# RWKV layers: loras ahead of the last keys, receptances and token products ahead of the block solution, values beside it, blocks written one by one

## The chip, the cores and the metric

The kernel runs on one core of one Trainium2 chip. The metric is the device time of an execution in microseconds (us); lower is better. The time before is the median of three runs. One further execution was taken by the hardware profiler, and all rows of a trace below are of that one.

The names of the engines in the rows: PE is TensorE (matrix products, and PEld its loads of weights), DVE is VectorE, ACT is ScalarE, POOL is GpSimd, SP is SyncE, which here does nothing but start the loads of weights. ACT and POOL also issue DMAs (transfers between the on-chip memory and DRAM).

## What is computed

A network of four layers and a second block on 256 tokens of width 1024, in float32. Each layer has a mixer between two SwiGLU parts. The mixers of layers 0 and 3 are RWKV time mixing, of layer 1 a Mamba2, of layer 2 an attention with a window. The change touches the two RWKV mixers alone. Cut to what matters:

```python
def rwkv7_time_mix(h, mu, w_rkv, w_o, w0, w1, w2, a0, a1, a2, g1, g2, ...):
    dx = token_shift(h) - h
    xr, xw, xk, xv, xa, xg = [h + dx * mu[j] for j in range(6)]
    r, k, v = xr @ w_rkv[0], xk @ w_rkv[1], xv @ w_rkv[2]
    w = -softplus(-(w0 + tanh(xw @ w1) @ w2)) - 0.5
    decay = exp(-exp(w))
    a = sigmoid(a0 + (xa @ a1) @ a2)
    # layer 3 alone: v += (v_first - v) * sigmoid(v0 + (xv @ v1) @ v2)
    g = sigmoid(xg @ g1) @ g2
    kk = heads(k * k_k); kk = kk / max(norm(kk), 1e-12)
    k = k * (1 + (a - 1) * k_a)
    ...
    def step(state, inp):          # 256 tokens, 16 heads of 64
        r_t, w_t, k_t, v_t, kk_t, a_t = inp
        sa = einsum('bhvk,bhk->bhv', state, -kk_t)
        state = state * w_t + sa (x) (kk_t * a_t) + v_t (x) k_t
        return state, einsum('bhvk,bhk->bhv', state, r_t)
    y = scan(step, ...);  y = group_norm(y)
    bonus = sum(rh * kh * r_k, axis=-1) * vh
    return ((y + bonus) * g) @ w_o
```

## The kernel before, in words

**Tiles.** The width of 1024 lies in eight tiles of 128 partitions (KT = 8), two heads in each. The tokens are cut into four chunks of 64. The recurrence over tokens is replaced by products in a chunk: within a chunk, each token's `sa` depends on those of the tokens before it, which is a triangular system, solved by blocks of 32 x 32. There are 2 blocks for each of 4 chunks and 16 heads: 128 blocks, one in each partition.

**The stages of an RWKV mixer** (`rwkv`, line 653), in the order in which they come: the keys (`pjrkv`), with the loras of decay and rate beside them (`lora_wa`, `lora_up`); then for each pair of tiles `ahead(k0)`, which is `directions` (the normed keys, `ss`, `KK`), `decay` (running sums `cs`) and `factors`. `factors` ends with the products `pd` of directions and keys, whose copy `tm` goes to DRAM as `dL`. `solve` reads the blocks back into `LT`, one block in a partition, inverts them in 31 steps of two DVE instructions each (`fs`, `LT`; lines 865 and 866), and sends the result by DRAM (`dTU`) into `T` and `U`. After that, lanes run: `inverse` (`px`, `pt`), `recur` (the states of one tile, chunk by chunk), and at the end the output product `rwo`.

The parts that the change moves: `receive(i)` is the receptance of a tile, a `whole` (line 695, one tile of output, eight matrix products over a weight of 512 KB, `raw`), multiplied into `R`; `values(k)` is the same for the values (`Vv`); `grams(k)` makes the products `pg` of a tile, masked by DVE into `GM`; `tokens(k)` turns a tile's data to token order (`tok`), makes the bonus (`rk`, `bo`) and the values in token order (`tokv`, `UV`); `gates` is the lora of the gate (`g1a`, `g1b`, `lgs`, then `g2a`, `g2b`).

**What sets the order.** Each part is a generator that yields now and then. `weave` (line 233) takes them round robin, one step each, and what they emit is the order of the instructions; each engine then runs its own in that order, and waits where one needs the result of another engine or a buffer. So a part that is woven in at another place moves on all engines. Before, these lines set it around the solution (`SOLVED` is 4, `VALUES` (2, 6)):

```python
weave([chain(ahead(0), ahead(4)), chain(repeat(None, 2), ahead(2), ahead(6)),
       chain(*(values(k) for k in range(VALUES[0]))), chain(repeat(None, 6), plain(0, xr))])
...
weave([solve(), fill, chain(repeat(None, SOLVED), gates()),
       chain(*(chain(grams(k), tokens(k)) for k in range(4)))])
```

`fill` holds the values 2 to 5 and receptances 0 to 3 in turn. The lanes then take receptances 4 to 7 and values 6 and 7 along, and `grams` and `tokens` of tiles 4 to 7. `plain(0, xr)` is the mix that receptances multiply, `plain(3, xv)` that of the values.

**Weights** come in the order of use through SP's queue into three buffers (`raw`), so a load waits until the third load before it has been used. The DMAs of `dL`, `dTU`, `T` and `U` are issued by ACT (`self.bounce`) and POOL.

## Time and profile before

| | us |
|---|---|
| median of 3 runs (3024.62 to 3029.52) | 3026.28 |
| profiled execution | 3033.78 |
| span of its trace | 3032.0 |

The span is the time from the first to the last instruction in the trace; the profiled execution lies 7.5 us above the median. A row of the page gives for each engine the time in which it was busy in this span; an engine that waits for another is not busy. Two mixers of the kind that is changed lie in the span, from about 220 to 480 us and from about 2030 to 2280 us with their output.

### The profile page before, as it was taken

The numbers are of one execution on the slowest core, as the hardware profiler recorded it, in microseconds if no ns is written. First come the engines' busy times: TensorE is split into PE (matmuls) and PEld (weight loads), VectorE is DVE, ScalarE is ACT, GpSimd is POOL, SyncE is SP. The second block draws the span as 40 slices with busy tenths as digits, with TensorE's granted clock in tenths as the row PEclk, the third lists the DMA queues.
The fourth block names the chain that finished last, engine by engine and source line by source line (L and its number), as shares of the span: only waits on it lengthen the run. The fifth ranks groups of instructions, "written<-read, shape, count | busy, mean of one in ns | idle before, by whom it ended". The sixth has DMA issues, their size and how long they took to land. (4 is left out here: it accounts for less than half of the span.)

```text
span 3032.0 us, 57166 instructions
## 1 busy us (share of the span) xinstructions
PE 2889.5 (95%) x23002; PEld 2729.8 (90%) x23002; DVE 2180.5 (72%) x3805; ACT 1553.4 (51%) x2697; POOL 77.1 (3%) x89
## 2 busy tenths in 40 slices
PE   7998799999998999999999999998799999999898
PEld 6997688999998989999988999996688999889898
DVE  8886425888788888888887888774536757566754
ACT  5546134545456765455466545444245446644543
POOL 0001100000001100000000000001000000000000
PEclk9999799999999999999999999999799999999999
DMA  9983313797884547888844897853314665544464
GB/s 323 337 312 89 96 60 103 258 305 268 302 271 160 161 154 232 285 286 280 296 150 143 310 311 250 296 198 95 90 55 127 210 181 181 174 145 126 155 186 133
DMA packets 185051, 613.36 MB, mean 202 GB/s; under 512 B 30353, under 2 KB 34321, under 8 KB 184786
## 3 DMA queue, kind: packets, MB, share of 16 engines
q1 hardware_dynamic: 168626, 595.49, 59.7%
q0 software_dynamic: 2816, 8.72, 0.9%
q10 hardware_dynamic: 13344, 5.51, 0.8%
q8 instruction: 180, 2.95, 0.4%
q14 instruction: 85, 0.70, 0.1%
HBM read 603.31 MB, written 6.32 MB: 201 GB/s over the span
## 5 line engine op out<-in xcount | busy, mean ns | idle before, releaser
L295 ACT ACTIVATE wh<-raw 128x1024 fp32r<-128x1024 f32 (+3 forms) x824 | 850.9, 1036 | 929.4 <-DMA raw<-in_wi 243.5
L374 DVE TENSOR_TENSOR wl<-raw,wh 128x1024 fp32r<-128x1024 f32 (+3 forms) x824 | 987.4, 1200 | 390.8 <-ACT wh L295 385.1
L383 PE MATMUL pjwi<-xl,wh 128*128 128x256 f32 x2568 | 722.3, 283 | 3.8 <-DVE xl L507 3.5
L382 PE MATMUL pjwi<-xh,wh 128*128 128x256 f32 x2568 | 716.2, 283 | 2.8 <-ACT xh L295 1.5
L384 PE MATMUL pjwi<-xh,wl 128*128 128x256 f32 x2568 | 716.4, 281 | 0.0
L383 PEld LDWEIGHTS pjwi<-xl,wh 128*128 128x128 f32 x2568 | 485.1, 189 | 6.0 <-DVE xl L507 5.8
L384 PEld LDWEIGHTS pjwi<-xh,wl 128*128 128x128 f32 x2568 | 486.1, 190 | 0.0
L382 PEld LDWEIGHTS pjwi<-xh,wh 128*128 128x128 f32 x2568 | 480.9, 189 | 3.6 <-ACT xh L295 1.9
L383 PE MATMUL pdwo<-gl,wh 128*128 128x256 f32 x1408 | 396.4, 282 | 0.0
L384 PE MATMUL pdwo<-gh,wl 128*128 128x256 f32 x1408 | 395.6, 281 | 0.0
L382 PE MATMUL pdwo<-gh,wh 128*128 128x256 f32 x1408 | 395.1, 281 | 0.0
L423 DVE SCALAR_TENSOR_TENSOR aring<-aring,cbc 128x1024 f32<-128x1024 f32 x286 | 343.5, 1221 | 2.7 <-DMA aring<-in_adaw 2.6
L382 PEld LDWEIGHTS pdwo<-gh,wh 128*128 128x128 f32 x1408 | 265.3, 188 | 0.0
L384 PEld LDWEIGHTS pdwo<-gh,wl 128*128 128x128 f32 x1408 | 265.2, 188 | 0.0
L383 PEld LDWEIGHTS pdwo<-gl,wh 128*128 128x128 f32 x1408 | 265.1, 188 | 0.0
L695 PE MATMUL whole<-mf,raw 128*128 128x256 f32 x512 | 129.7, 407 | 13.7 <-DMA raw<-in_rkv 13.4
L695 PEld LDWEIGHTS whole<-mf,raw 128*128 128x128 f32 x512 | 101.0, 203 | 36.6 <-DMA raw<-in_rkv 15.9
L383 PE MATMUL pjw2i<-xl,wh 128*128 128x256 f32 x416 | 119.1, 287 | 0.0
L384 PE MATMUL pjw2i<-xh,wl 128*128 128x256 f32 x416 | 118.1, 284 | 0.0
L382 PE MATMUL pjw2i<-xh,wh 128*128 128x256 f32 x416 | 117.3, 282 | 0.1
L382 PE MATMUL pjmbi<-xh,wh 128*128 128x256 f32 x352 | 101.8, 293 | 4.5 <-ACT shc L295 2.1
L383 PE MATMUL pjmbi<-xl,wh 128*128 128x256 f32 x352 | 101.9, 291 | 0.0
(526 smaller groups left out, 5681.2 us busy)
## 6 DMA issues: line engine op xcount, KB each, us to landing
raw<-in_wi SPq DMA_DIRECT2D x352, 512.0 KB, 4.7
aring<-in_adaw SPq DMA_DIRECT2D x286, 512.0 KB, 5.3
raw<-in_wo SPq DMA_DIRECT2D x128, 512.0 KB, 4.8
raw<-in_w2i SPq DMA_DIRECT2D x56, 512.0 KB, 4.1
raw<-in_wo SPq DMA_DIRECT2D x64, 384.0 KB, 4.5
raw<-in_rkv SPq DMA_DIRECT2D x48, 512.0 KB, 3.7
raw<-in_mbi SPq DMA_DIRECT2D x48, 512.0 KB, 3.7
raw<-in_fg SPq DMA_DIRECT2D x22, 512.0 KB, 4.3
```

Source lines behind the costliest of these rows:

```text
L295: ins = self.nc.scalar.activation(out, in_, func, **k)
L374: self.last = self.nc.vector.tensor_tensor(lo, src, hi.bitcast(F32), SUB)
L382: mm(out, a, xh[:parts, k, :], start=start, stop=False)
L383: mm(out, a, xl[:parts, k, :], start=False, stop=False)
L384: mm(out, b, xh[:parts, k, :], start=False, stop=stop)
L423: ins = nc.vector.scalar_tensor_tensor(raw, raw, 1.0, self.cbc, MUL, MUL, accum_out=m[:, b % 24:b % 24 + 1])
L695: mm(ps[:, :T], w[:, k * P:k * P + P], x[0][:, k, :], start=k == 0, stop=k == KT - 1)
```

## The change

It moves work between the stages and changes the way of the blocks through DRAM; the amount of matrix work is the same.

- The loras of decay and rate, in layer 3 also that of the values, are woven from the start of the last keys, before them in each round, and yield less often. The mix for the receptances (`xr`) is made beside the keys as well.
- `ahead` of all four pairs is woven together, each starting two rounds after the one before, and beside it stand values 0 and 1, receptances 0 to 3, and `grams` and `tokens` of tiles 0 to 3. `tokens` no longer needs the values: it copies the product `bo` over `rk` and keeps it.
- Beside the solution stand values 2 to 7, the gates' lora and a new part, `bonus(k)`, that makes `tokv`, `UV` and the bonus of tiles 0 to 3.
- The lanes take receptances 4 to 7 along, no values.
- `dL` is laid out by blocks. Each pair writes eight pieces (32 partitions, four blocks' rows of 128 bytes each), four from ACT and four from POOL, where it was two from ACT with rows of 1 KB. `LT` is read by two DMAs of 64 partitions (4 KB in a row), where it was eight, with rows of 128 bytes.

```diff
--- before.py
+++ after.py
@@ -23,9 +23,8 @@
 EARLY = 2
 QB = 8
 STAGGER = (0, 1, 2, 3)
-SOLVED = 4
-VALUES = (2, 6)
-BURSTS = 3
+VALUES = 2
+BURSTS = 1
 START = 6
 AHEAD = 7
 IDLE = (1, 1, 3, 1, 1, 1)
@@ -719,7 +718,8 @@
             for k in range(KT):
                 mm(ps[:, :T], w[:, k * P:k * P + P], h[:, k, :], start=k == 0, stop=False)
                 mm(ps[:, :T], ws[k // 4][:, k % 4 * P:k % 4 * P + P], dx[:, k, :], start=False, stop=k == KT - 1)
-                yield
+                if k % 2:
+                    yield
             act(t[:64], ps[:64, :T], AF.Tanh)
             act(t[64:], ps[64:, :T], AF.Copy)
             yield
@@ -744,7 +744,7 @@
                     ps = self.ax("up")
                     mm(ps[:, :T], w[r, k * P:k * P + P], t[0][r], start=True, stop=True)
                     act(dst(k), c8(ps[:, :T]), AF.Sigmoid, bias=self.p(bias, k))
-                if k % 2 or len(ups) > 1:
+                if k % 2:
                     yield
 
         def project(n, x, done):
@@ -771,7 +771,7 @@
         SC, rest = self.small("SC", 4 * KT, 1), self.small("rest", 8, 1)
         SC = SC.rearrange("p (k c) -> p k c", c=4)
         V.tensor_scalar(rest, self.p(f"k_a{j}", 0, 8), -1.0, 1.0, MUL, ADD)
-        dL = self.dp.tile([2 * KT, 64 * T + 64], F32, name=f"dL_{l}")
+        dL = self.dp.tile([2, 4, KT, 2, 32, 32], F32, name=f"dL_{l}")
         dTU = self.dp.tile([2, 2, 32, 2, 1024], F32, name=f"dTU_{l}")
         KK, IP = self.b8("KK"), self.b8("IP")
         b2 = lambda name: self.sp.tile([P, 512], F32, tag="b2", name=name, bufs=3)
@@ -808,6 +808,7 @@
             act(SC[:, sl, :3], sc, AF.Exp, scale=-DECAY)
             V.scalar_tensor_tensor(c8(sg)[:, :, 1:], c8(kk)[:, :, 1:], -1.0, c8(e)[:, :, :63], MUL, MUL)
             V.scalar_tensor_tensor(c8(sg)[:, :, 0], c8(kk)[:, :, 0], -1.0, first, MUL, MUL)
+            decayed.update(range(k0, k0 + 2))
             yield
 
         def factors(k0):
@@ -832,8 +833,11 @@
             yield
             tm = b2("tm")
             act(tm, pd, AF.Copy)
-            for h_, r in enumerate(H2):
-                self.bounce.dma_start(dL[2 * k0:2 * k0 + 4].rearrange("(k h) x -> h k x", h=2)[h_, :, :64 * T].rearrange("k (s c) -> s k c", c=T), pair(tm)[r])
+            for n in range(4):
+                h_, i = divmod(n, 2)
+                for d, k in enumerate(ks):
+                    queues[(n + d) % 2].dma_start(dL[k // 4, :, 2 * (k % 4) + h_, i].rearrange("c s t -> s c t"),
+                                                  c8(pair(tm)[32 * n:32 * n + 32, d])[:, :, 32 * i:32 * i + 32])
             factored.update(ks)
             yield
 
@@ -843,13 +847,10 @@
             L, Tm = LT[:, 0], LT[:, 1]
             t3 = Tm.rearrange("p (i j) -> p i j", j=32)
             l3 = L.rearrange("p (i j) -> p i j", j=32)
-            queues = self.bounce, nc.gpsimd
             for half in range(2):
                 while len(factored) < 4 * half + 4:
                     yield
-                for c in range(4):
-                    o = 64 * half + 16 * c
-                    queues[c % 2].dma_start(l3[o:o + 16], dL[8 * half:8 * half + 8].rearrange("q (b x) -> (q b) x", b=2)[:, :32 * T].rearrange("g (i x) -> g i x", x=T)[:, :, 64 * c:64 * c + 32])
+                queues[half].dma_start(L[64 * half:64 * half + 64], dL[half].rearrange("c g i s t -> (c g i) (s t)"))
             V.memset(Tm, 0.0)
             V.memset(Tm[:, 0:1024:33], 1.0)
             U.append(self.b8("U", F32, (P, 32, 64)))
@@ -894,17 +895,25 @@
             yield
 
 
-        Vv, valued = self.b8("Vv"), set()
+        Vv, valued, decayed, factored = self.b8("Vv"), set(), set(), set()
+        queues = self.bounce, nc.gpsimd
         self.table(TABLE_SIGM)
-        loras = [lora_wa(lwa), lora_up("wa2", (j,), P, lwa, [(H2[0], f"w0{j}", lambda k: c8(SG[:, k])), (H2[1], f"a0{j}", Aa)])]
-        weave([keys, chain(*loras), plain(3, xv)])
+        lows, ups = [lora_wa(lwa)], [lora_up("wa2", (j,), P, lwa, [(H2[0], f"w0{j}", lambda k: c8(SG[:, k])), (H2[1], f"a0{j}", Aa)])]
         if j:
-            finish(chain(lora("v1", (j - 1,), xv, 32, AF.Copy, lv), lora_up("v2", (j - 1,), 32, lv, [(slice(0, 32), "v0", lambda k: c8(Vv[:, k]))])))
+            lows.append(lora("v1", (j - 1,), xv, 32, AF.Copy, lv))
+            ups.append(lora_up("v2", (j - 1,), 32, lv, [(slice(0, 32), "v0", lambda k: c8(Vv[:, k]))]))
+        mixes = chain(plain(3, xv), plain(0, xr))
+        if j:
+            for _ in range(4):
+                next(mixes)
+        weave([chain(*lows, *ups), keys, mixes])
         self.table(TABLE_NORM)
         hc = lambda t, h_: t[:, 64 * h_:64 * h_ + 64]
-        received, factored, solved, ready, U, GMs, UVs = set(), set(), [], set(), [], {}, {}
+        received, solved, ready, U, GMs, UVs, bos = set(), [], set(), [], {}, {}, {}
 
         def receive(i, tag, steps=2):
+            while i not in decayed:
+                yield
             ps = yield from whole(0, i, xr, tag, steps)
             V.tensor_tensor(R[:, i], R[:, i], ps, MUL)
             received.add(i)
@@ -926,7 +935,6 @@
                 yield
 
         ahead = lambda k0: chain(directions(k0), decay(k0), factors(k0))
-        weave([chain(ahead(0), ahead(4)), chain(repeat(None, 2), ahead(2), ahead(6)), chain(*(values(k) for k in range(VALUES[0]))), chain(repeat(None, 6), plain(0, xr))])
         def inverse(k):
 
             while not solved:
@@ -949,20 +957,27 @@
 
         def tokens(k):
 
+            rk = self.b1("rk")
+            V.scalar_tensor_tensor(c8(rk), c8(R[:, k]), self.p(f"r_k{j}", k), K(k), MUL, MUL)
+            pt = self.ax("tok")
+            both = AK[k // 4][:, k % 4].rearrange("p c q t -> p (c q t)")
+            for c in range(4):
+                nc.tensor.transpose(pt[:, P * c:P * c + P], both[:, P * c:P * c + P], ident)
+            act(both, pt, AF.Copy)
+            yield
+
+            bo = self.ax("bo")
+            mm(bo[:, :T], blk, rk, start=True, stop=True)
+            bos[k] = rk
+            act(rk, bo[:, :T], AF.Copy)
+            yield
+
+        def bonus(k):
+
             half = k // 4
             top, bot = H2[half], H2[1 - half]
             while k not in valued:
                 yield
-            rk = self.b1("rk")
-            V.scalar_tensor_tensor(c8(rk), c8(R[:, k]), self.p(f"r_k{j}", k), K(k), MUL, MUL)
-            bo = self.ax("bo")
-            mm(bo[:, :T], blk, rk, start=True, stop=True)
-            pt = self.ax("tok")
-            both = AK[half][:, k % 4].rearrange("p c q t -> p (c q t)")
-            for c in range(4):
-                nc.tensor.transpose(pt[:, P * c:P * c + P], both[:, P * c:P * c + P], ident)
-            act(both, pt, AF.Copy)
-            yield
             if half not in UVs:
                 UVs[half] = self.b8("UV", F32, (P, 4, 512))
                 nc.gpsimd.memset(UVs[half][top], 0.0)
@@ -970,8 +985,7 @@
             for c in range(4):
                 mm(pv[bot, P * c:P * c + P], Vv[:, k, 64 * c:64 * c + 64], C["cen"], start=True, stop=True)
             act(UVs[half][bot, k % 4], pv[bot], AF.Copy)
-
-            V.tensor_tensor(Vv[:, k], bo[:, :T], Vv[:, k], MUL)
+            V.tensor_tensor(Vv[:, k], bos.pop(k), Vv[:, k], MUL)
             yield
 
         def recur(k, sts):
@@ -1066,9 +1080,11 @@
             self.table(TABLE_NORM)
             yield
 
-
-        fill = chain(*(p for k in range(4) for p in ([values(k + VALUES[0])] if k + VALUES[0] < VALUES[1] else []) + [receive(k, "mm")]))
-        weave([solve(), fill, chain(repeat(None, SOLVED), gates()), chain(*(chain(grams(k), tokens(k)) for k in range(4)))])
+        fill = chain(*(values(k) for k in range(VALUES)), *(receive(k, "mm") for k in range(4)))
+        weave([chain(repeat(None, k0), ahead(k0)) for k0 in range(0, KT, 2)] + [fill, chain(*(chain(grams(k), tokens(k)) for k in range(4)))])
+
+        fill = chain(*(values(k) for k in range(VALUES, KT)))
+        weave([solve(), fill, gates(), chain(*(bonus(k) for k in range(4)))])
         ST = self.b8("ST", F32, (P, 8, P))
         nc.gpsimd.memset(ST, 0.0)
         wg1, wg2 = self.get("g2a", (j,), 0, 1024, 128), self.get("g2b", (j,), 0, 1024, 32)
@@ -1092,11 +1108,8 @@
         sts = lambda n: (ST[:, 2 * n], ST[:, 2 * n + 1])
         lanes = [chain(repeat(None, s), inverse(n), recur(n, sts(n)), recur(n + 4, sts(n))) for n, s in enumerate(STAGGER)]
 
-        bursts = [receive(i, "ax", KT) for i in range(4, KT)]
-        for n, k in enumerate(range(VALUES[1], KT)):
-            bursts.insert(2 * n + 1, values(k, KT, "ax"))
-        rs = chain(*(chain(b, repeat(None, BURSTS - 2)) for b in bursts))
-        weave(lanes + [rs, chain(*(chain(grams(k), tokens(k), inverse(k)) for k in range(4, KT)))] + [closing(k) for k in range(0, KT, 2)] + [splits()])
+        rs = chain(*(chain(receive(i, "ax", KT), repeat(None, BURSTS)) for i in range(4, KT)))
+        weave(lanes + [rs, chain(*(chain(grams(k), tokens(k), bonus(k), inverse(k)) for k in range(4, KT)))] + [closing(k) for k in range(0, KT, 2)] + [splits()])
         m = self.mod(l, 1)
         finish(self.output(lambda i: ("rwo", (j, i)), Y, m))
 
```

The rows below are of the order of instructions in layer 0, before and after; a row is line, operation, result<-operands, shape and count.

PE before, from the third of four `pd` to the second `pg`; `whole` on `mf` are receptances and values, `lora` the gates' lora:

```order
L831 MATMUL pd<-SR,AK 64x64 x16
L695 MATMUL whole<-mf,raw 128x256 x10
L831 MATMUL pd<-SR,AK 64x64 x16
L733 MATMUL lora<-dx,raw 128x256 x8
L924 MATMUL pg<-SR,AK 128x128 x8
L733 MATMUL lora<-dx,raw 32x256 x8
L695 MATMUL whole<-mf,raw 128x256 x28
L959 MATMUL bo<-rk,cbase 128x256
L963 MATMUL tok<-cbase,AK 128x128 x4
L971 MATMUL tokv<-crw,Vv 64x128 x4
L924 MATMUL pg<-SR,AK 128x128 x8
```

The gates' lora stands among the first `pg`, 28 products of values and receptances ahead of the first `tok`. PE after, at the same place:

```order
L832 MATMUL pd<-SR,AK 64x64 x16
L694 MATMUL whole<-mf,raw 128x256 x16
L832 MATMUL pd<-SR,AK 64x64 x16
L933 MATMUL pg<-SR,AK 128x128 x8
L965 MATMUL tok<-cbase,AK 128x128 x4
L970 MATMUL bo<-rk,cbase 128x256
```

Now `pg`, `tok` and `bo` of a tile stand right behind the last `pd`, those of three more tiles behind them, with no lora among them.

PE after, in the second half of the solution and behind it, up to the first `pt` of the lanes (`pc` belongs to `recur`):

```order
L733 MATMUL lora<-dx,raw 32x256 x4
L986 MATMUL tokv<-crw,Vv 64x128 x4
L694 MATMUL whole<-mf,raw 128x256 x32
L1011 MATMUL pc<-UV,GM 64x64 x8
L948 MATMUL px<-T_3386,GM 32x32 x8
L694 MATMUL whole<-mf,raw 128x256 x8
L953 MATMUL pt<-U,X_3658 32x32 x8
```

The lora of the gates and the values stand now beside the solution and are done ahead of `px`, but for one `whole`.

ACT before, from the copy of the third pair's `pd` to the reads of the blocks (`DMA` is an issue, `ka` a factor of the next pair):

```order
L295 ACTIVATE tm<-pd 128x512
L295 ACTIVATE ka<-AK,rest,par 128x256
L836 DMA dL_2763<-tm 64x2x256 x2
L295 ACTIVATE ka<-AK,rest,par 128x256
L852 DMA LT<-dL_2763 16x32x32
L287 ACT_TABLE_LOAD
L295 ACTIVATE tm<-pd 128x512
L295 ACTIVATE Vv<-whole 128x256
L836 DMA dL_2763<-tm 64x2x256 x2
L295 ACTIVATE g1a<-lora 128x256
L852 DMA LT<-dL_2763 16x32x32 x2
```

Behind the last two stores stands one copy, then two reads.

ACT after, at the same place:

```order
L294 ACTIVATE ka<-AK,rest,par 128x256
L286 ACT_TABLE_LOAD
L294 ACTIVATE Vv<-whole 128x256
L294 ACTIVATE tm<-pd 128x512
L839 DMA dL_2759<-tm 32x4x32 x4
L294 ACTIVATE AK<-tok 128x512
L294 ACTIVATE rk<-bo 128x256
L294 ACTIVATE AK<-tok 128x512
L294 ACTIVATE rk<-bo 128x256
L853 DMA LT<-dL_2759 64x1024
```

Two stores have become four, and the read of half of the blocks stands behind the copies of two tiles' `tok` and `bo`.

## Rows read from the trace of the kernel before

**Rows 1.** The page: busy time of each engine, share of the span, instructions.

```profile
PE 2889.5 (95%) x23002; PEld 2729.8 (90%) x23002; DVE 2180.5 (72%) x3805; ACT 1553.4 (51%) x2697; POOL 77.1 (3%) x89
```

**Rows 2.** Stretches, layers 0, 3: length, PE, PEld, DVE, ACT, POOL busy, PEclk, DMA, GB/s.

```profile
265.80:308.70 42.90, 33.89 (x238) 26.15 (x236) 31.09 (x58) 21.45 (x43) 11.26 (x11) 0.93 0.36 99
308.70:323.60 14.90, 14.90 (x75) 11.46 (x76) 2.50 (x6) 3.90 (x8) 4.27 (x5) 0.98 0.56 156
323.60:353.50 29.90, 13.62 (x74) 11.21 (x73) 26.82 (x74) 4.06 (x7) 0.56 (x1) 0.77 0.28 87
353.50:376.00 22.50, 22.50 (x106) 18.07 (x103) 4.46 (x9) 4.00 (x8) 3.81 (x5) 0.54 0.34 74
376.00:476.40 100.40, 100.40 (x905) 81.88 (x904) 32.36 (x78) 40.01 (x112) 2.88 (x3) 0.95 0.17 52
...
2069.00:2112.50 43.50, 34.64 (x238) 25.76 (x237) 32.68 (x66) 23.38 (x47) 12.78 (x9) 0.92 0.38 100
2112.50:2127.10 14.60, 14.60 (x75) 11.22 (x76) 2.47 (x6) 3.36 (x6) 1.27 (x2) 1.00 0.61 144
2127.10:2158.90 31.80, 15.52 (x69) 12.78 (x68) 27.78 (x77) 3.58 (x5) 1.71 (x3) 0.68 0.28 90
2158.90:2176.30 17.40, 16.97 (x111) 13.72 (x109) 6.24 (x14) 4.21 (x8) 4.95 (x7) 0.80 0.46 110
2176.30:2276.00 99.70, 99.70 (x884) 81.56 (x884) 34.70 (x84) 38.39 (x106) 1.80 (x1) 0.93 0.17 53
```

**Rows 3.** Timeline of PE: start, length, work, in brackets idle time before and its end.

```profile
294.08 1.13 PE L695 MATMUL whole<-mf,raw 128*128 128x256 f32 x4 [2.71 <-DMA raw<-in_rkv]
...
304.35 2.43 PE L695 MATMUL whole<-mf,raw 128*128 128x256 f32 x8 [3.68 <-DMA raw<-in_rkv]
```

**Rows 4.** Groups of DVE, 323.6 to 353.5: busy, mean ns | idle time before.

```profile
L865 DVE TENSOR_TENSOR fs<-LT 128x31 f32<-128x31 f32 (+15 forms) x31 | 10.6, 342 | 1.0
L866 DVE TENSOR_TENSOR LT<-LT,fs 128x31 f32<-128x31 f32 (+15 forms) x31 | 10.6, 341 | 0.9
L374 DVE TENSOR_TENSOR wl<-raw,wh 128x1024 fp32r<-128x1024 f32 (+1 forms) x2 | 2.4, 1212 | 0.0
...
L925 DVE TENSOR_TENSOR GM<-pg,crw 128x512 f32<-128x512 f32 x2 | 1.4, 683 | 0.0
L869 DVE COPY LT<-LT 128x1024 f32<-128x1024 f32 x1 | 1.1, 1054 | 0.0
...
L974 DVE TENSOR_TENSOR Vv<-bo,Vv 128x256 f32<-128x256 f32 x1 | 0.4, 425 | 1.3 <-PE tokv L971 1.3
```

**Rows 5.** Timeline of PE: a `whole` at low clock, then work at full clock.

```profile
370.82 5.29 PE L695 MATMUL whole<-mf,raw 128*128 128x256 f32 x16
...
2167.28 1.74 PE L924 MATMUL pg<-SR,AK 64*128 64x128 f32 x16
...
2170.15 0.66 PE L963 MATMUL tok<-cbase,AK 128*128 128x128 f32 x4 [0.23 <-DVE GM L925]
2170.74 1.09 PE L971 MATMUL tokv<-crw,Vv 128*64 128x128 f32 x8
2171.75 0.69 PE L940 MATMUL px<-T,GM 32*32 32x32 f32 x16
2172.63 3.72 PE L695 MATMUL whole<-mf,raw 128*128 128x256 f32 x16
```

**Rows 6.** Tile views of `tm` (first two rows) and `dL`: min/median/max, ns of an issue, us to landing.

```profile
L836 ACTq DMA_DIRECT2D dL<-tm x16: 582/597/667, 277.1 to 2113.8; - x16
...
DMA to landing us min/median/max: 2.4/2.5/4.8
...
DMA to landing us min/median/max: 2.2/3.6/5.5
```

**Rows 7.** Timeline of POOL: the issue that reads T.

```profile
355.24 0.82 POOL L877 DMA_DIRECT2D T<-dTU  x1
```

**Rows 8.** DMA issues from 300 to 370: KB each, median us from issue to landing.

```profile
T<-dTU POOLq DMA_DIRECT2D x1, 128.0 KB, 4.5
```

## The prediction

> **What bounds the kernel now.** I read the page first: over the whole span TensorE (PE) is busy 95% of the time, the vector engine (DVE) 72%, the scalar engine (ACT) 51% [rows 1]. By that alone a change of order could win little; but the change touches only the two RWKV layers, and there the share is another. So I cut the two stretches into stages, at the instructions that end them (the timeline gives the marks): **A** from the first `ss` to the last `pd` (directions, decay, factors), **B** from there to the first step of `solve`, **C** the solution until the copy of `LT` has ended, **D** from there to the first `pt` of the lanes, **E** the lanes until `rwo` begins. In [rows 2] five rows are layer 0, five layer 3; the second column is the length of the stage, the third PE's busy time.
>
> In A PE is busy 33.9 of 42.9 us, in C 13.6 of 29.9; in layer 3 34.6 of 43.5 and 15.5 of 31.8. PE is thus idle for some 25 us a layer. In D it is busy throughout but at a granted clock of 0.54 (0.80 in layer 3), so that its work there takes nearly double. Only E is bound by PE, at 0.95 and 0.93. Next, the reasons, from PE's timeline: within A it waits for a key or receptance weight (`raw<-in_rkv`) 2.71 us at 294 and 3.68 at 304 [rows 3]. C is bound by DVE: its 31 steps are 10.6 + 10.6 us, the copy 1.1 [rows 4], of 26.8 busy.
>
> **The change, stage by stage.** The total of the matrix work stays; what changes is beside which other work it stands.
>
> *A.* Here DVE is busy 31.1 and ACT 21.5 of 42.9 us [rows 2], so neither fills it; the weights' waits and the chain through DVE do. After, the `g1a` and `g1b` loads stand behind ten rkv loads, not between them, so they hold no raw buffer during A, and the receptances' weights come in time. The order has 55 products of `whole` in place of 50 in this stage (one `whole`, a tile of output, is eight products, one for each tile of the input). A product is two records of the trace; a `whole`, 16 records, is 3.72 us at full clock [rows 5], 0.46 a product; I take 0.44, as they lie close to each other here. The sum is PE's busy time plus 5 x 0.44: 33.9 + 2.2 = 36.1 and 34.6 + 2.2 = 36.8, so -6.8 and -6.7. The two waits for weights are 6.4 us in layer 0, which is nearly this. DVE loses the receptances' mixes to the phase of the keys (there PE is the busy one) and gains two `R` products and four `rk`; it stays near 30, under 36.
>
> *B.* 14.9 and 14.6 us now: the gate loras and a product, all PE. They go to C. In their place stand four heads of `grams` and `tokens`: `pg` 1.74, `tok` 0.66 [rows 5] and `bo`, one product, 0.46, so 4 x 2.86 = 11.4, and one `GM` of DVE, 0.68 [rows 4], behind it: 12.1. The other chain of B is the way of the blocks: the copy `tm`, taken like an issue at 0.6, four issues on ACT of 0.6, landing 2.5 [rows 6], the read's issue 0.6 and its landing. That read of `dL` is new in form (rows of 4 KB, 64 partitions). The landings that bound it are the stores' 2.5 and the longest of `dL`, 5.5, which is a present read in pieces of 128 bytes, since the stores end at 4.8 [rows 6]: 8.6 to 11.6 us with it, in both cases below 12.1. So B is 12.1: -2.8 and -2.5.
>
> The new stores write pieces of 128 bytes where the old wrote 1 KB. The trace has for 128-byte pieces up to those 5.5 us, in reads, against 2.5 for the stores [rows 6]. If they land like those reads, the chain is 11.6 to 14.6 us and B at worst 14.6, 2.5 over my value; I take 2.5 us, the landing of stores, and keep the other for the upper end. The Trainium skill ("DMA: Bandwidth & Descriptors", Specifications) says that below 512 bytes a transfer falls under line rate, since the engine reads, modifies and writes. By that rule the stores would come under the dearer case, and the sum be -42 instead of -47.
>
> *C.* The steps and the copy stay: 21.2 + 1.1. Between them stood 4.5 us of other DVE work (26.8 less 22.3); in the order after stand four `Vv` products of 0.42, a `GM` of 0.68, two `lgs` like `Vv` and a split of a weight, 1.21 [rows 4]: 4.4. Of the idle time, 29.9 - 26.8 = 3.1, 1.9 is ahead of the steps themselves [rows 4] and stays. So 28.6, -1.3; layer 3, whose values bring more for DVE, I put at 30.8, -1.0. What PE gets here must fit: `tokv` 4 x 1.09 = 4.4 [rows 5], 16 lora products 7.4, 39 products of `whole` 17.2, together 29 us at full clock, as long as the stage; the 6 us in which D waits for T are the reserve. This is the cover for the moved work: if PE stands at half clock there (now 0.77, 0.68), the last values end up to 25 us later, in front of `px`.
>
> *D.* Now 22.5 and 17.4: T is read 1.7 us after the copy's end [rows 7] and lands after 4.5 [rows 8], at 359.7, but PE is still at half clock in `grams`, `tokens` and products, and `px` stands behind these. After, only `pc` and one `whole` stand there. 1.7 + 4.5 + `px` 0.7 and the `whole` at low clock, 5.3 us [rows 5], are 12.2: -10.3 and -5.2.
>
> *E.* Values 6 and 7 leave the lanes: two `whole`s of 3.7 [rows 5], and PE is busy throughout: -7.4 in each layer.
>
> *ACT and POOL.* Instead of 8 stores and 4 reads ACT issues 16 stores and a read, POOL the other 16 stores. One issue is 0.6 us [rows 6]. Nothing, if it falls into ACT's idle half of A; 8 x 0.6 = 4.8 if each of eight more lies in the chain from `tm` to `ka` of the next pair. I take 2 for each layer, the middle, as ACT idles half of A.
>
> **Sum.** Layer 0: -6.8 - 2.8 - 1.3 - 10.3 - 7.4 = -28.6. Layer 3: -6.7 - 2.5 - 1.0 - 5.2 - 7.4 = -22.8. Plus 4: -47.4. The profiled execution took 3033.78 us (its span 3032.0), 7.5 above the median of 3026.28; against it 2986.4, on the median 2979.
>
> **Rivals.**
>
> *The lanes don't shrink.* For it: in E the chain from `px` over `pt` to the states passes between DVE and PE in each lane, and DVE and ACT are busy 32 and 40 of 100 us. Against: PE has no idle time there. If both `whole`s merely filled gaps, 14.8 comes back: 2994.
>
> *PE stays cold.* Between C's work and `px` PE has only `pc` for some 6 us; after the idle stretches of C, 16 us in all, it was granted 0.54 in D. If E's first 22.5 us run so (0.54 for 0.95), some 10 us come back in each layer: about 3000. For it: D now. Against: only 6 us, with `pc` in it. The Trainium skill ("TensorE: Matmul & The Clock Gate", Part 1) says that idleness throttles the clock and sustained work releases it; D agrees, with its 0.54.
>
> *The stores hold ACT up: slower.* After, most stores of `dL` wait, by the order, for a DMA issued some eight DMAs earlier, weight loads included, and behind them on ACT stand `SR`, `ka` and `sq` of the next pairs, for which DVE and PE wait. If each waits x us, A is 21.5 + 12x (ACT's busy time and its stores in A), 23.4 + 12x in layer 3, and the chain of B (0.6 + 4x + 2.5 + 0.6 + some 4) is 4x - 4.4 longer than 12.1. Set against A's 36.1 and 36.8 and the mean gain of 25.7 per layer, it decides from 16x - 18.4 = 25.7, x = 2.75. At the median landing of `dL`, 3.6 [rows 6], a layer is some 13 us longer than now, 3053. For it: 2.75 lies within the landings. Against: eight DMAs earlier is mostly long landed by then.
>
> **Numbers.** My forecast has 0.58 and its own range, 2960 to 2995; the lanes' rival 0.13, the cold PE 0.13, the stores 0.16, of which 0.06 for small waits that leave it within 0.2% (6 us, about what a measurement can tell) and 0.10 for slower. So faster 0.84, same 0.06, slower 0.10. The low end: no issue costs (-4), the `whole` after `px` at full clock (5.29 to 3.72, twice: -3), E at full clock (0.05 and 0.07 of 100 us: -12): 2960. The high end: E gains nothing (+14.8), eight issues in the chain (+5.6), the read of `dL` in B 2.5 late in each layer (+5), and C 3 us longer for late products (+6): 3010. Below lies 0.04, above the stores' 0.16.
>
> **What would show it.** Right: no wait for `raw<-in_rkv` in A, which ends about 36 us after its start; the first step follows the last `pd` by about 12; C is filled with PE at a clock near 1; `px` follows the copy by 6 to 7. Wrong: dL's stores on ACT far apart, in front of idle DVE and PE; a solution that waits for `LT` after the `GM` are done; the values' `whole`s in front of `px`; lanes as long as before with idle PE.

## The result and the profile after

| | before | after |
|---|---|---|
| median, us | 3025.45 (4 runs, 3021.96 to 3029.52) | 3044.6 (4 runs, 3042.72 to 3046.63) |
| ratio, 95% interval | | 1.0063 [1.0045, 1.008] |
| profiled execution, us | 3033.78 | 3042.72 |

The change made the kernel slower by 0.6%; 2979 was forecast. The profiled execution of before lies 8.3 us above its median, that of after 1.9 below, so the two traces show only 8.9 us of the 19.2 between the medians. What is said of sizes below goes by the medians of the experiments where there is one.

The page of after, the line that answers to [rows 1]:

```profile
PE 2907.3 (96%) x23002; PEld 2740.7 (90%) x23002; DVE 2176.8 (72%) x3805; ACT 1557.4 (51%) x2713; POOL 88.9 (3%) x115
```

PE has as many instructions as before and is busy 17.8 us longer: the same work at a lower granted clock, over the whole span 0.963 of the full one, before 0.970. The stretches of after are cut at the same marks A to E as [rows 2], and a sixth, F, goes from the first `pjrwo` to the last. Columns: length; busy time of PE, PEld, DVE, ACT, POOL (x: instructions); PEclk, the granted clock as a share of the full one; DMA share; GB/s. Layer 0 comes first:

```profile
271.40:306.20 34.80, 32.62 (x248) 26.01 (x246) 25.34 (x46) 21.89 (x43) 14.44 (x19) 1.00 0.42 114
306.20:316.30 10.10, 10.10 (x89) 8.62 (x88) 5.51 (x10) 3.21 (x7) 5.63 (x8) 1.00 0.31 80
316.30:347.50 31.20, 30.09 (x158) 23.47 (x156) 25.63 (x71) 9.25 (x17) 3.96 (x6) 1.00 0.36 106
347.50:365.30 17.80, 7.58 (x37) 6.02 (x38) 1.21 (x1) 1.36 (x5) 5.27 (x6) 0.62 0.65 200
365.30:465.60 100.30, 100.30 (x831) 79.42 (x830) 31.91 (x77) 39.15 (x110) 0.00 (x0) 0.83 0.13 38
465.60:519.60 54.00, 50.65 (x341) 43.06 (x340) 24.13 (x51) 21.33 (x47) 0.00 (x0) 0.83 0.33 107
...
2078.60:2113.70 35.10, 32.64 (x248) 26.04 (x246) 26.83 (x53) 21.20 (x40) 13.51 (x17) 1.00 0.40 110
2113.70:2123.40 9.70, 9.70 (x83) 8.22 (x84) 6.01 (x12) 3.21 (x7) 6.44 (x8) 1.00 0.31 68
2123.40:2155.50 32.10, 30.19 (x152) 23.28 (x151) 26.86 (x78) 8.39 (x14) 3.68 (x6) 1.00 0.43 126
2155.50:2171.20 15.70, 8.63 (x45) 6.92 (x45) 4.57 (x11) 0.65 (x2) 4.73 (x5) 0.57 0.62 180
2171.20:2271.70 100.50, 100.50 (x832) 79.66 (x831) 31.91 (x77) 39.17 (x110) 0.00 (x0) 0.83 0.14 42
2271.70:2329.50 57.80, 55.08 (x340) 47.23 (x340) 23.00 (x45) 21.80 (x46) 0.00 (x0) 0.73 0.28 88
```

A to D are shorter in both layers. The loss is in E and F, which must be read together, since the order now sets the first `pjrwo` earlier among the lanes' products. Before they were 145.4 us (376.0 to 521.4) and 143.9 (2176.3 to 2320.2; the E of [rows 2] ends 3.3 us ahead of layer 3's first `pjrwo`); now 154.3 and 158.3, with two `whole`s less in each. The clock tells where: 0.83 in E, 0.83 and 0.73 in F, where before it was 0.95 and 0.93 [rows 2] in E. E and F as one stretch, before, layers 0 and 3:

```profile
376.00:521.40 145.40, 143.98 (x1208) 119.99 (x1208) 56.40 (x128) 60.07 (x154) 2.88 (x3) 0.93 0.24 75
2176.30:2320.20 143.90, 143.24 (x1208) 119.32 (x1208) 57.80 (x129) 60.66 (x153) 1.80 (x1) 0.93 0.23 72
```

And after:

```profile
365.30:519.60 154.30, 150.95 (x1171) 122.49 (x1170) 56.03 (x128) 60.49 (x156) 0.00 (x0) 0.83 0.20 62
2171.20:2329.50 158.30, 155.58 (x1170) 126.89 (x1170) 54.91 (x122) 60.98 (x155) 0.00 (x0) 0.80 0.19 59
```

The length times the clock, an estimate of the length at full clock, is 135 and 134 us before and 128 and 127 after: some 7 us less in each layer, as much as two `whole`s. So the work did leave E and F, and the lower clock more than ate it.

Two smaller losses lie ahead of A. Layer 3's keys with their loras, from the first `lora` to the first `ss`, take 53.0 us, before 47.3; and from the last `pdwo` to the first `lora` it is 10.9 and 6.9 us, before 5.8 and 5.0. DVE's timeline of after at the start of layer 0 (start, length, work, idle time ahead):

```profile
223.18 1.23 DVE L373 TENSOR_TENSOR wl<-raw,wh 128x1024 fp32r<-128x1024 f32 x1 [2.20 <-ACT wh L294]
224.78 0.69 DVE L717 TENSOR_TENSOR wmu<-raw,par 128x512 f32<-128x512 f32 x1 [0.38 <-DMA raw<-in_wa]
225.39 0.48 DVE L574 SCALAR_TENSOR_TENSOR xT<-pdwo,mod,xT 128x256 f32<-128x256 f32 x1
```

The last update of the residual (`xT`), on which the norm waits, now stands behind `wmu`, the scaled weight of the first lora, and `wmu` behind that weight's load; in the order of before it stands ahead of it. But `wmu` waits for its load for 0.38 us and takes 0.69, about 1 us of the 5.1 in layer 0; where the rest arises is not shown.

### The profile page after: what moved, and what is told of

The parts are those of the page before. It is cut to its first block, busy times and chain, and to the rows that moved or that the text cites. A ratio compares the mean times of both kernels' runs of the same rounds, so it can differ in the third digit from the quotient of the medians.

```text
span 3040.9 us, 57272 instructions
## 1 busy us (share of the span) xinstructions
PE 2907.3 (96%) x23002; PEld 2740.7 (90%) x23002; DVE 2176.8 (72%) x3805; ACT 1557.4 (51%) x2713; POOL 88.9 (3%) x115
```

## The experiments

A first theory: six `whole`s had kept PE's clock up in the lanes; the last now ends at 401 us (the expectation below has 404), before at 442, and PE then falls to half clock. The rival: lanes and output are paced by their own chain. Four runs. Before, run again beside all the experiments, had medians from 3023.26 to 3025.47 us, so that their medians can be set against that of after.

**Values 6 and 7 back in the lanes** (in all diffs below "-" is after, where not said otherwise):

```diff
-        fill = chain(*(values(k) for k in range(VALUES, KT)))
+        fill = chain(*(values(k) for k in range(VALUES, KT - 2)))
...
+        for n, k in enumerate(range(KT - 2, KT)):
+            bursts.insert(2 * n + 1, values(k, KT, "ax"))
```

> After, with the whole products of values 6 and 7 put back among the receptances in the lanes, at the places they had before. Clock theory: the lanes and the output product are 8.9 us longer than before in layer 0 and 14.4 in layer 3 since the last whole ends at 404 us, not at 444, and PE then falls to half clock; with six wholes again the granted clock from 430 to 490 us is near that of before (1.00 and 0.83 in two windows of 30 us, 0.71 and 0.66 after) and the time falls by some 23 us, to 3018 to 3025. Rival, that the lanes and the output are paced by their own chain of small products and weights, whatever else PE does: 3040 to 3048.

Measured 3043.29 (ratio to before 1.0056 [1.0037, 1.0075]): no change from after. With all six `whole`s in the lanes the clock fell all the same, to 0.51 from 437 to 488 us. The theory falls in this form. Lanes and output (E and F) became 10.4 us longer in both layers together, but stage D became 11.8 and 10.9 us (17.8 and 15.7 in after), of which more below.

**Products that do nothing, in place of the values**:

```diff
+        def warm():
+            ps = self.ax("warm")
+            for k in range(KT):
+                mm(ps[:, :T], blk, self.xT[:, k, :], start=k == 0, stop=k == KT - 1)
+            yield
...
+            bursts.insert(2 * n + 1, warm())
```

> After, with two bursts of eight more matrix products (a constant matrix times the residual, 128x256 each, result not used) at the two places in the lanes from which values 6 and 7 were taken; nothing else is changed, no load, no vector work. Clock theory: more work makes it faster: the clock stays up as before, and the lanes and the output lose 15 to 23 us, 3022 to 3030. Rival 1, lanes bound by PE's work: 7.4 us more in each layer, 3059. Rival 2, lanes paced by their own chain: no change, 3042 to 3048.

Measured 3053.97 (1.0078 [1.0054, 1.0102]): 9.4 us more than after, for 14.8 of work at 3.7 a burst, with overlapping intervals. In its trace E and F are 166.6 and 162.8 us at clocks of 0.81 and 0.82, 16.8 more than in after in all. So early work in the lanes did not bring the clock back; whether it costs two thirds of its length or all of it is not clear.

**Receptances farther apart** (`BURSTS` 4 for 1).

> After, with four idle rounds behind each receptance in the lanes where it was one, so that the four wholes lie farther apart and end later; work and loads are the same. Clock theory: half clock begins later, and the time falls by some 5 to 12 us, 3033 to 3040, unless the gaps between the wholes are now long enough for the clock to fall in them. Rival, own chain: tiles 4 to 7 get their receptances later and the lanes end later, 3045 to 3060.

Measured 3038.92 (1.0044 [1.0026, 1.0062]); 5.7 us less than after, with overlapping intervals: not clear.

**Loras as before**:

```diff
-        weave([chain(*lows, *ups), keys, mixes])
+        weave([keys, chain(*lows, *ups), chain(plain(3, xv), plain(0, xr))])
+        if j:
+            finish(chain(lora("v1", ...), lora_up("v2", ...)))
```

> After, with the loras woven as before (behind the keys in each round, a yield for each product, layer 3's lora of the values behind the keys); the rest of the change stays. Theory: in the order after, the first scaling of the lora weight (wmu) stands in DVE's row ahead of the last update of the residual, and waits for a weight; the norm, and all of the layer, starts 5.1 us later in layer 0 and 1.9 in layer 3, and layer 3's keys with both loras are 5.9 us longer. All three come back: 3029 to 3035. Rival, the gaps are the weights' loads themselves, in whatever order: 3042 to 3048.

Measured 3031.7 (1.0016 [0.9997, 1.0035]), 12.9 less than after. In its trace layer 3's keys are 47.2 us and the way to its first `lora` is 5.0, as before, and so in all later runs with the loras as before (47.2 to 48.0, 5.0 to 5.1). In layer 0 that way was 5.7 here, but between 6.7 and 10.9 us in most others with either order; how much of the 12.9 stands there is not shown.

**A new theory of the lanes.** The order has 32 groups of the chain's product `pc<-r,U` in a layer, one for each of eight tiles and four chunks. In before 24 stand ahead of the last `px` and 8 behind it, in after 26 and 6. (Counts in the expectations below were summed wrongly: 22 for before and 20 for one yield less are both 24; 18 for two chains is 15, and 18 for one yield less again is 21.) The reason is in the diff: `tokens` and `bonus` together yield once more than the old `tokens`, and tiles 4 to 7 go through `grams`, `tokens`, `bonus`, `inverse` one after the other, so the last tile comes four rounds of the weave later. Its recurrence then runs at the end with little beside it.

**One yield less for tiles 4 to 7**:

```diff
             act(rk, bo[:, :T], AF.Copy)
-            yield
+            if k < 4:
+                yield
```

> After, with one yield less in each of the tiles 4 to 7 of the lanes: tokens goes on into bonus in the same round of the weave, as the undivided tokens did before. No instruction is added or removed, only the order of the lanes moves: the last px stands behind 20 chain products r,U pairs fewer or more as before (22 groups ahead of it in before, 26 in after, 20 here). New theory, the serial part of tiles 4 to 7 (grams, tokens, bonus, inverse, one tile after the other) sets the pace, and its extra round per tile puts the last px four chain steps later, so that the last tile's recurrence runs alone at the end, at half clock: the lanes with the output get back to 145 and 144 us or less, -9 to -16 and -14 to -21: 3008 to 3022. Rival, the missing wholes and the clock: 3040 to 3048.

Measured 3013.6 (0.9954 [0.9933, 0.9974]): 31 us less than after, by one line that adds or removes no instruction. The order has 24 groups ahead of the last `px`.

**The converse on the kernel before** ("-" is nothing here; a line is added behind `tokens`' last yield):

```diff
             yield
+            if k >= 4:
+                yield
```

> The kernel before, with one empty yield more at the end of tokens for tiles 4 to 7, and nothing else. The order then has 26 chain groups ahead of the last px, as after has, with the six wholes where they were. Theory of the extra round: the lanes with the output are 9 to 20 us longer in each layer, 3040 to 3055. Rival, the clock kept by the wholes: they are all there, so no change, 3020 to 3030.

Measured 3047.55 (1.0079 [1.0065, 1.0093]), 23.7 more than before (3023.82 beside it), with 26 groups ahead of the last `px`. Both lines point the same way. PE's timeline of after, rows of the chain around the last `px` (start, length, work; four records of `pc<-r,U` are a group):

```profile
451.44 0.68 PE L1016 MATMUL pc<-r,U 64*64 64x64 f32 x4
456.94 0.69 PE L1016 MATMUL pc<-r,U 64*64 64x64 f32 x4
461.49 0.69 PE L1016 MATMUL pc<-r,U 64*64 64x64 f32 x4
463.15 0.84 PE L948 MATMUL px<-T,GM 32*32 32x32 f32 x12
...
471.42 1.11 PE L1016 MATMUL pc<-r,U 64*64 64x64 f32 x8
```

The same rows of the run with one yield less:

```profile
449.10 0.69 PE L1017 MATMUL pc<-r,U 64*64 64x64 f32 x4
455.02 0.44 PE L1017 MATMUL pc<-r,U 64*64 64x64 f32 x4
455.39 0.69 PE L948 MATMUL px<-T,GM 32*32 32x32 f32 x16
456.38 0.44 PE L1017 MATMUL pc<-r,U 64*64 64x64 f32 x4
459.75 0.44 PE L1017 MATMUL pc<-r,U 64*64 64x64 f32 x4
461.84 0.67 PE L1017 MATMUL pc<-r,U 64*64 64x64 f32 x8
```

A group of four records takes 0.44 us at full clock and 0.69 at half. In after, from 451 to 472 the groups stand 4.6 to 9.9 us apart at half clock; with one yield less five stand between 455 and 463. E and F of that run, layers 0 and 3:

```profile
362.80:503.70 140.90, 139.46 (x1171) 115.32 (x1170) 56.73 (x128) 60.48 (x156) 0.00 (x0) 0.90 0.21 68
2150.80:2297.20 146.40, 145.72 (x1171) 119.75 (x1171) 55.95 (x123) 61.21 (x156) 0.00 (x0) 0.85 0.20 64
```

PE has the same number of instructions as in after, and the length times the clock is 127 and 124 us, much as there (128 and 127): the run is faster by a higher clock. It is still below the 0.93 of before, and so the two `whole`s that left make E and F only 2.0 us shorter than before in all.

**Both mends together** (one yield less, loras as before).

> Both mends: the loras as before and one yield less for tiles 4 to 7; the rest of the change stays (products ahead of the solution, values beside it, blocks written one by one). If both costs are separate they add: 3031.7 less 23 to 36, 2996 to 3009, faster than before by 0.5 to 0.9 per cent. If the lanes don't gain: 3028 to 3035.

Measured 2997.81 (0.9915 [0.989, 0.994]): 46.8 less than after, 26.0 less than before (3023.82). The mends add: 31.0 and 12.9 alone are 43.9.

**Two chains for tiles 4 to 7**, beside each other, on top of both mends:

```diff
-... + [rs, chain(*(chain(grams(k), tokens(k), bonus(k), inverse(k)) for k in range(4, KT)))]
+... + [rs, *(chain(*(chain(grams(k), tokens(k), bonus(k), inverse(k)) for k in ks)) for ks in ((4, 6), (5, 7)))]
```

> The last, with the serial part of tiles 4 to 7 in two chains, 4 and 6 beside 5 and 7. The order has 18 chain groups ahead of the last px, where it is 20 with one chain. If the serial part still sets the pace, the recurrences of the last tiles run side by side and the time falls by another 5 to 20 us from the run with both mends. If PE's work or the recurrence of a lane is the bound by then, it is the same within 0.2%, or some us more, as the tail has no other work left to go beside it.

Measured 3017.27 (0.9976 [0.9954, 0.9998]): slower by 19.5 than one chain, with 15 groups ahead of the last `px`. That the last `px` comes as early as possible is therefore not what counts. In its trace E and F are 150.3 us at a clock of 0.81 and 158.4 at 0.75.

**Idle products at the end of the lanes of after**, two in a round for the last sixteen rounds:

```diff
+        def warm():
+            ps = self.ax("warm")
+            for k in range(2):
+                mm(ps[:, :T], blk, self.xT[:, k, :], start=k == 0, stop=k == 1)
+            yield
...
+        rs = chain(..., repeat(None, 9), *(warm() for _ in range(16)))
```

> After, with 32 more products in each layer (a constant matrix times the residual, result not used), two in a round, in the last sixteen rounds of the lanes, where after has half clock; the extra step per tile stays. This asks how the extra step costs its 13 us: by time that the chain needs at any clock, or since the end of the lanes is so thin that PE falls to half clock, where a chain step takes 4.6 us (after, 442 to 493 us) and not 3.6 (before, 442 to 496). If the clock is a part: the clock in 440 to 490 us is near 1 and the time falls by 5 to 20 us although work is added, 3025 to 3040. If the steps take as long at any clock, the products lie in the chain or beside it: 3045 to 3075.

Measured 3019.91 (0.9986 [0.9963, 1.0009]): 24.7 us less than after, with 32 products more in each layer and nothing moved. Layer 0 from 430 to 490 us, columns as above, for after:

```profile
430.00:460.00 30.00, 30.00 (x202) 23.42 (x202) 10.37 (x25) 10.37 (x28) 0.00 (x0) 0.71 0.01 1
460.00:490.00 30.00, 30.00 (x192) 23.37 (x189) 6.26 (x17) 9.85 (x28) 0.00 (x0) 0.66 0.01 3
```

The same stretch of after with the idle products:

```profile
430.00:460.00 30.00, 30.00 (x234) 22.95 (x233) 10.43 (x26) 12.45 (x35) 0.00 (x0) 1.00 0.01 1
460.00:490.00 30.00, 30.00 (x222) 22.43 (x221) 6.65 (x18) 9.19 (x25) 0.00 (x0) 1.00 0.03 6
```

Of these PE instructions so many are idle products (length, busy time, clock, DMA share, GB/s):

```profile
430.00:460.00 30.00, 6.95 (x24) 1.00 0.01 1
460.00:490.00 30.00, 11.44 (x40) 1.00 0.03 6
```

The clock rose from 0.71 and 0.66 to 1.00, but PE was busy 30 of 30 us in both, and without the 64 idle ones it got through 392 instructions in place of 394. E and F of that trace:

```profile
362.30:515.70 153.40, 151.52 (x1237) 122.66 (x1237) 57.66 (x130) 61.31 (x156) 0.00 (x0) 0.94 0.20 63
2165.00:2321.40 156.40, 156.40 (x1235) 126.21 (x1235) 55.30 (x123) 61.74 (x157) 0.00 (x0) 0.90 0.18 60
```

The length times the clock is 144 and 141 us, 16 and 14 more than in after: the idle work costs its length, and here the clock gave back that and 2.8 us more. This trace is of the slowest of the run's twelve executions (3033.26); in which stages the other executions win the 24.7 of the medians is not shown. But the mean clock is 0.974 to 0.980 in all twelve, and 0.960 to 0.963 in the four of after. So the extra round costs, for a good part at least, by the lower clock of a thin end; how much of its 24 to 31 us is not shown. The Trainium skill ("TensorE: Matmul & The Clock Gate", Part 1) says that idleness throttles the clock and sustained work releases it. This run agrees by its mean clocks, though the work is useless, but not in every stretch: in layer 3 of its trace the clock was 0.63 from 2230 to 2260. And PE counts as busy throughout at 0.71 and 0.66 in after, so busy time does not show such idleness.

**The same products with two chains**, from the fifth round behind the last receptance.

> The run with two chains, with 28 more such products in each layer in the rounds near the end of its lanes. Two chains were 19 us slower than one, at a clock of 0.67 and 0.50 in 430 to 490 us, where one chain has 0.89 and 1.00. If that is the clock, it comes back to 2996 to 3010 with the products. If the two chains cost by themselves (a lane's recurrence bound, or buffers), 3017 to 3040.

Measured 3021.59 (0.9993 [0.9971, 1.0014]): no gain. In its trace layer 3's lanes with the output took 143.8 us at clocks of 0.95 and 1.00, but layer 0's 162.1 at 0.61 and 0.63. Why the clock is lower with two chains is not settled by it.

**Values 6 and 7 in the lanes, with both mends.**

> The kernel with both mends (loras as before, one yield less), with values 6 and 7 back in the lanes. With values beside the solution, four weight loads of 512 KB run while its result goes through DRAM, and the first T is read 5 us later (landing of dTU 6.0 and 7.6 us against 2.6 and 3.3 before); that goes: -10. The lanes get two wholes each: at 3.7 us +14.8 if PE is their bound, +9 by the run with dummy products. 2993 to 3003, so no clear difference; below 2993 if the lanes hide the wholes.

Measured 2997.27 (0.9914 [0.988, 0.9948]), the same as without. D's cost was expected from the DMA view; `dTU` carries the solution out. The DMA view of after, 345 to 366 us (KB, median us to landing):

```profile
raw<-in_rkv SPq DMA_DIRECT2D x4, 512.0 KB, 5.5
dTU<-LT ACTq DMA_DIRECT2D x1, 512.0 KB, 6.0
dTU<-LT POOLq DMA_DIRECT2D x1, 512.0 KB, 7.6
```

That of the first run above, with values 6 and 7 in the lanes and no mend, 336 to 358 us:

```profile
raw<-in_rkv SPq DMA_DIRECT2D x4, 512.0 KB, 3.9
dTU<-LT ACTq DMA_DIRECT2D x1, 512.0 KB, 2.6
dTU<-LT POOLq DMA_DIRECT2D x1, 512.0 KB, 3.1
```

In after four weights of 512 KB are loaded just then. In the run with the values in the lanes no bytes move from 343.2 to 345.3, where `dTU` is issued (344.7): the loads ahead of it have landed. There D is 6.0 and 4.8 us shorter than in after. With both mends it is 17.3 and 11.1 us without the values in the lanes, 11.6 and 11.4 with them: there the loads cost D 5.7 us in layer 0 and nothing in layer 3, and two `whole`s more in the lanes take back what is won.

**The way of the blocks as before, with both mends** (two stores a pair, eight reads).

> The kernel with both mends, with the way of the blocks as before (two stores of a pair, rows of 1 KB, eight reads with pieces of 128 bytes). By the prediction the way is hidden in either form behind grams and tokens, and ACT's issues cost 0 to 4.8 us a layer: 2990 to 3000. If the new form is what lets the solution start 10 us behind the last pd, the old reads (up to 5.5 us to land) hold the first step: 3000 to 3010.

Measured 3003.53 (0.9936 [0.9912, 0.996]), 5.7 more, intervals overlapping. From the last `pd` to the first step it is 14.9 and 18.9 us, with the new form 10.3 and 9.7: the old form would not have been hidden. Its E and F, layers 0 and 3:

```profile
366.60:496.80 130.20, 128.86 (x1170) 106.86 (x1170) 56.61 (x128) 60.15 (x156) 0.00 (x0) 0.99 0.23 74
2145.70:2289.40 143.70, 143.02 (x1171) 118.49 (x1171) 55.84 (x123) 61.04 (x156) 0.00 (x0) 0.87 0.21 66
```

In one execution and with as many instructions, layer 0 takes 13.5 us less than layer 3, at a clock of 0.99 against 0.87; the length times the clock is 129 and 125 us.

**One yield less again** (`bonus` goes on into `inverse`), with both mends.

> The kernel with both mends, with one more yield less for each of the tiles 4 to 7 (bonus goes on into inverse in the same round). The order has 18 chain groups ahead of the last px, where the mended has 20 and after 26. If the place of the last px is what counts, whatever else: 2980 to 2993. If what counts is that the end of the lanes has enough work at full clock, an earlier last px leaves other lanes' steps for the end, as with two chains, and gains little or loses: 2994 to 3017.

Measured 3007.71 (0.9955 [0.9934, 0.9975]), 9.9 more than with one, with intervals that just overlap; 21 groups ahead of the last `px`.

**One yield less in before.**

> The kernel before with one yield less in tokens for tiles 4 to 7: the converse of the run with one more, which cost 24 us. If the pace of the serial part is the bound in before too: 3005 to 3018. If before already stands at the best place, as the wholes and the tail are balanced there: 3019 to 3035.

Measured 3028.63 (1.0017 [0.9993, 1.0042]): no gain; 22 groups. With 15, 21 and 22 groups, each in a kernel of its own, nothing is won against 24; 26 costs 24 to 31 us. Of the places tried none is better than the one at which before stood.

**Only layer 3's lora of the values as before, with one yield less.**

> After with one yield less, and of the loras only layer 3's lora of the values as before (behind the keys); those of decay and rate stay ahead of the last keys. All loras as before gave 13 to 16 us. If it is layer 3's keys with two loras between them (53.0 us to 47.3) and no more: 3013.6 less 6, 3005 to 3010. If it is the place of wmu ahead of the residual, in both layers: 3010 to 3016, and the layers still begin 7 to 11 us behind the last product.

Measured 3004.53 (0.9939 [0.9916, 0.9961]): 9.1 less than with one yield less alone, of 15.8 that all loras give, with overlapping intervals. Layer 3's keys are 47.5 us, but 6.5 lie ahead of its loras, where it is 5.0 with all loras as before. So the lora of the values among layer 3's keys costs those keys some 6 us by the traces; the share of the medians is not clear. The rest goes with the other loras; that `wmu` ahead of the residual is all of it was not tried alone, and its row, with about 1 us in layer 0, speaks against it.

## Why the prediction was wrong

**The step that failed is E**: "Values 6 and 7 leave the lanes: two `whole`s of 3.7 [rows 5], and PE is busy throughout: -7.4 in each layer". It took E for work at a rate, and counted which work leaves. The work was right: by length times clock E and F are some 7 us shorter in each layer. The rate was wrong: the step took the clock of E to stay at its 0.95 and 0.93, and over E and F it fell from 0.93 in both layers to 0.83 and 0.80. So E and F are +8.9 and +14.4 by the traces, in place of -14.8 in all, a miss of 38 us. The step did not count the rounds: the split of `tokens` gives each of tiles 4 to 7 one more, and by the runs that costs 31 us (one yield less) or 24 (one more in before). That it costs by the clock is shown by the same work at 0.83 and 0.80 with the round and 0.90 and 0.85 without it; why a thinner end is granted less is argued from the rows and from the idle products, and the run without the round still won only 2.0 of the 14.8. The rival "PE stays cold" had the mechanism but the wrong end of the lanes, and "the lanes don't shrink" left out a loss.

**Ahead of A** the prediction had no term at all: the loras were named as moved and cost at nothing, without the work that hides it. By the medians they cost 12.9 to 15.8 us.

**D** had the right chain and a wrong size: T's way at 1.7 + 4.5 us, from an execution with few loads beside it. It came to -4.7 and -1.7 by the windows, not -10.3 and -5.2: in layer 0 `px` started 10.7 us after the copy's end, not 6.2, and the `whole` behind it took 6.2 us, not 5.3 (at full clock it is 3.72, so neither is the "nearly double" that the prediction says of D). PE's timeline of after:

```profile
358.16 1.03 PE L948 MATMUL px<-T,GM 32*32 32x32 f32 x16 [9.49 <-DMA T<-dTU]
359.12 6.21 PE L694 MATMUL whole<-mf,raw 128*128 128x256 f32 x16
```

**A** was right: -8.1 and -8.4 for -6.8 and -6.7; one wait for `raw<-in_rkv` is left in each layer, 0.63 and 0.75 us, and the clock is 1.00. **B** was right in sign and small: -4.8 and -4.9 for -2.8 and -2.5, as the first step is set between the last two `GM`. **C** is +1.3 and +0.3 for -1.3 and -1.0; PE's work fits at a clock of 1.00, but `Vv` stands between the steps and waits 3.7 us in layer 0 for `tokv`, `vf` and `UV`. **The stores** hold up little: 9.5 us of waits on ACT, DVE and POOL are put down to `dL` in both layers together. The tile view of `dL` in after (min/median/max: ns of an issue on ACT, us to landing):

```profile
L839 ACTq DMA_DIRECT2D dL<-tm x32: 309/420/459, 282.1 to 2115.7; - x32
...
DMA to landing us min/median/max: 1.4/3.3/4.4
```

ACT issues one in 0.42 us, not 0.6, and stores and reads of `dL` land within 4.4. The dearer case for which the Trainium skill ("DMA: Bandwidth & Descriptors", Specifications) spoke did not come in B, which took 10.1 and 9.7 us. But a store is now 16 KB, an eighth of one before, and lands no sooner: after 3.4 us, where it was 2.5. The stages A to D together gained 31.0 us by the windows (110.2 less 93.9 in layer 0, 107.3 less 92.6 in layer 3), where 32.6 were forecast with the issues: the sum over them was right, and in part by luck: A and B gave 7.4 us more than forecast and the issues' 4 did not come, while C and D gave 13.0 less.

## What to carry to other kernels

Where a weave sets the order, count rounds and not only work: one yield more in the part that all lanes wait for added or removed no instruction, and cost 24 to 31 us, about what four stages gained (31.0). A PE that is "busy" all the time may be so at half clock, and then busy time does not tell what can be won; look at the length times the granted clock of each stretch, and at what is left to run beside the last lane. Work that is taken out can cost more clock than it saves. When work is pulled ahead, look also at what its first instruction now stands in front of.

## What the hardware showed that was not expected

Executions of one kernel lie up to 30 us apart: one yield less from 2988.94 to 3019.24 us, before from 3014.97 to 3045.61. The fast ones have the higher clock: in one yield less the fastest has a mean of 0.977, the slowest 0.968. Lanes and output of the mended order took 130.2 us at a clock of 0.99 and 143.7 at 0.87 in one execution. Adding 32 products a layer that nobody reads made the kernel 24.7 us faster by its median. And two DMAs of 512 KB that landed in 2.6 and 3.1 us took 6.0 and 7.6 beside four others of that size, at up to 437 GB/s in the view of that stretch.
